# A new pace for the sample's gathered rows in both expert stages of a one-core encoder step: products, value sets, one row load and one copy stand at other places in the order

## The chip, the cores and the metric

The kernel runs on one core of one Trainium2 chip. The metric is device microseconds (us) of one launch; lower is better. Times of the profiled execution come from one trace. The engines are TensorE (PE: matmuls; PEld: its weight loads), VectorE (DVE), ScalarE (ACT), GpSimd (POOL, which here issues the gathers and a few row loads) and SyncE (SP, which issues the plain loads of the tables).

## The reference, cut to what matters

A two-layer encoder runs one step for a prompt of 256 frames and for a sample of 8 x 16 = 128 frames. Each layer is a mixer (a state-space scan in the first, windowed attention in the second) followed by `peer`, a retrieval over 16384 experts. The change is in `peer`:

```python
q = xn @ w_q                                   # 8 heads, two halves of 128
s1, s2 = q_half1 @ sub_k1.T, q_half2 @ sub_k2.T
...                                            # top 16 of each, top 16 of their sums
eid = e1 * 128 + e2                            # 8 x 16 = 128 experts a token
gate = softmax(vs)
ue = take(u_tab, eid)                          # (128 tokens, 128 experts, 1024)
act = gelu(einsum('tkd,td->tk', ue, x))
ve = take(v_tab, eid)
out = einsum('tk,tkd->td', gate * act, ve)
```

## The kernel before, in words

`peer(l)` runs twice, once for each layer. It treats the two token sets in different ways.

**The 256 prompt tokens go through all experts densely.** The tables `u_t` and `p_v` stream through once, a tile of 128 x 1024 f32 (512 KB) a step. There are 256 steps, which I number s = 0 to 255: s = 0 to 63 are the first half of u, s = 64 to 127 the second half, s = 128 to 255 the values v. In a u step (`u_step`) PE multiplies the tile with the prompt's activations, and ACT writes the result's GELU to `G[0]` or `G[1]`, a buffer of 64 expert columns for each half. Nearly every tile is split in two first (`split`): ACT rounds it (`hi`), DVE subtracts (`lo`), and PE makes three products of 8 matmuls (lines 144 to 146), 24 in a u step. A v step (`v_step`) has 12 matmuls of 512 columns (line 157), and its column of G is split as well (`phi`, `plo`). Some steps of the first half of u and of v run unsplit (lines 1188 and 1235). The gates are scattered into G by `w_step`, every second step from s = 64 to 191: DVE makes the masks `ob` (L1201), `og` (L1204) and half of `oa` (L1217), ACT the other half (L1214, L1215), PE does 16 small matmuls (L1221), and DVE multiplies the result into G (L1223).

**The 128 sample tokens fetch their own experts' rows.** There are 128 items in u. For each, POOL issues a gather of 512 KB (`fetch_u`, L1122) into one of three buffers `gath`, and DVE multiplies it with the tokens' rows and sums (`u_item`, L1160, called "the product" below). The products come in four groups of 32; each group needs the activations' rows in another arrangement, which `load_group(g)` (L946) brings from memory: groups 0 and 2 into the one buffer `xg`, groups 1 and 3 into columns of G that are free by then. A group's end (L1148, L1166) turns its 32 sums into coefficients. In v there are 32 sets of four rows: POOL gathers each row (`fetch_v`, L1122, into free columns of G), DVE makes a mask (`cm`, L1173) and PE adds the set with eight matmuls (`v_quad`, L1179), two for each of the four 32-column positions of the array.

**What sets the order.** All engines run their own instructions in a fixed order. A scheduler chooses it by its own simulated times when the kernel is built, and `pin` keeps some instructions in the order in which the code gives them. The code asks for the sample's work at each step: `tick(s)` makes products until as many are done as `U_DUE` wants by step s, with straight lines between its points, and for each it first fetches the row of the item after next; `quads(s)` makes the sets that `V_DUE` lists up to s, and then fetches rows for the next ones. `load_group(1)` stands at the turn of the halves (s = 64), `load_group(2)` behind item 31 and `load_group(3)` at v step 35 (s = 163). Before all this `peer` turns the normed activations and splits them (`qhi`, `qlo`), and ACT makes an unsplit copy `xf` (L931) for the unsplit steps.

Of the kernel before, what the change touches and what calls it, by code (L numbers as in the profile page):

```python
# [19 lines left out]
P = 128  # L20
# [35 lines left out]
U_DUE = ((64, 30), (128, 72), (192, 110), (216, P))  # L56
V_DUE = [72 + 7 * i for i in range(6)] + [148 + int(4.4 * i) for i in range(10)] + [193 + int(3.6 * i) for i in range(16)]
# [4 lines left out]
def encoder_step(ctx: ExitStack, tc: tile.TileContext, t_in, t_out):  # L62
# [825 lines left out]
    def peer(l):  # L888
        with ExitStack() as c:
# [35 lines left out]
            xf = T(xfctx.__enter__(), [P, KD, NP], F32, tag="xf")  # L925
            for k in range(KD):
                ps = bank([P, NT])
                for b in range(NB):
                    pe.transpose(ps[:, b * P:(b + 1) * P], xn[b][:, k * P:(k + 1) * P], ident)
                split(qhi[:, k], qlo[:, k], ps, scale=gcol[:, 2 + l, k:k + 1])  # L930
                act.activation(xf[:, k], ps[:, :NP], AF.Copy, scale=gcol[:, 2 + l, k:k + 1])  # L931
# [7 lines left out]
            def load_group(g):  # L939

                if g % 2:
                    xg[g] = (G[1][:, HE - 4:] if g == 1 else G[0][:, 32:36]).rearrange("p e t -> p (e t)")
                else:
                    xg[g] = T(one, [P, D], F32, tag="xg", bufs=1)
                rows = xrow[g]
                pool.dma_start(xg[g], bass.AP(tensor=rows.tensor, offset=rows.offset, ap=[[0, GR], [D, TG], [1, D]]))  # L946
# [184 lines left out]
            def fetch_v(n, s):  # L1131

                half, e = (1, HE - 20 + 4 * (n % 4)) if s < 2 * HE else (0, 4 * (n % v_bufs(s)))
                assert all(k != (half, e) for k, _ in vrows.values())
                tile_ = G[half][:, e:e + 4].rearrange("p e t -> p (e t)")
                r, q = divmod(n, 4)
                vrows[n] = (half, e), gather(tile_, t_in["p_v"], eidT[:, 32 * q + r:32 * q + r + 1])
# [17 lines left out]
            def u_item(k):  # L1155
                g, j = divmod(k, TG)
                if j == 0:
                    au[g] = T(one, [P, TG], F32, tag="au", bufs=1)
                tile_ = urows.pop(k)
                pin(dve.scalar_tensor_tensor(tile_, tile_, 1.0, xg[g], op0=OP.mult, op1=OP.mult,  # L1160
                                             accum_out=au[g][:, j:j + 1]))
                if j == TG - 1:
                    if g == 0:
                        load_group(2)
# [102 lines left out]
            def quads(s):  # L1267
# [8 lines left out]
                for _ in range(2):  # L1276
# [41 lines left out]
            for e2 in range(HE):  # L1318
# [4 lines left out]
                if e2 >= 4:  # L1323
                    quads(HE + e2)
# [5 lines left out]
            for e2 in range(2 * HE):  # L1330
                v_step(e2)
                if e2 == 35:
                    load_group(3)
# [127 lines left out]
```

## Time and profile before

| | us |
|---|---|
| three runs | 2552.58, 2550.56, 2542.86 |
| median | 2550.56 |
| the profiled execution, its own time | 2552.02 |
| its span, first to last instruction | 2550.1 |
| PE busy in the span | 2431.2 (95%) |
| DVE busy | 1883.9 (74%) |
| ACT busy | 1243.5 (49%) |
| POOL busy | 701.3 (27%) |

In the profiled execution `peer` of the first layer has its turn of the halves near 682 us, its v steps from about 919 to 1384 us. In the second layer the turn is near 1838 us, and the v steps run from about 2073 to 2536 us. A stretch's row gives the busy time of each engine there, the granted TensorE clock as a share of full speed, and the rate of the DMA engines. A row of the timeline gives start, length, engine, line, operation, tiles, and in brackets the engine's idle time ahead of it and what ended that.

### The profile page before, as it was taken

How to read it: one execution, taken by the hardware profiler on the slowest of the kernel's cores; microseconds unless marked ns; L12 is line 12 of the kernel's file. 1: busy time of each engine (PE TensorE's matmuls, PEld its weight loads, DVE VectorE, ACT ScalarE, POOL GpSimd, SP SyncE). 2: the span in 40 equal slices, each digit the busy share in tenths (PEclk: the TensorE clock that was granted, in tenths of full speed). 3: DMA queues.
4: the chain of work that ended last, by engine and by line, in shares of the span. 5: the costliest groups of instructions: out<-in, count | busy, mean ns of one | idle time of the engine just before them, and what ended most of it. 6: DMA issues, size and time to landing. Idle time of an engine off the chain costs nothing.

```text
span 2550.1 us, 44494 instructions
## 1 busy us (share of the span) xinstructions
PE 2431.2 (95%) x16655; PEld 2036.9 (80%) x16656; DVE 1883.9 (74%) x4163; ACT 1243.5 (49%) x2406; POOL 701.3 (27%) x755
## 2 busy tenths in 40 slices
PE   8999999999999999999999998999989999999998
PEld 7899978999888986656666878999978886656676
DVE  5888737979877788677655676978868787777655
ACT  5655524433555665554344554433546565554343
POOL 2222200022333224346432100022423224346431
PEclk9999999999999999999999999999989999999999
DMA  5545434477888889889996324477889889899995
GB/s 193 177 170 191 151 127 147 156 250 258 277 298 301 267 281 347 299 326 381 360 339 194 132 95 142 148 246 252 261 286 331 265 283 334 310 343 362 367 332 212
DMA packets 179768, 649.77 MB, mean 255 GB/s; under 512 B 23824, under 2 KB 25728, under 8 KB 176896
## 3 DMA queue, kind: packets, MB, share of 16 engines
q1 hardware_dynamic: 99936, 365.85, 41.0%
q0 software_dynamic: 79616, 281.08, 31.5%
q8 instruction: 130, 2.13, 0.3%
q14 instruction: 86, 0.70, 0.1%
HBM read 630.62 MB, written 18.06 MB: 254 GB/s over the span
## 4 chain that ended last, share of the span: by engine, by line
PE 75%; DVE 11%; DMA 6%; issue 4%; ACT 2%; POOL 1%; another core or an unknown queue 0%; SPq 0%; POOLq 0%; ACTq 0%; DVEq 0%
PE bank L157 25%; PE bank L146 10%; PE bank L144 10%; PE bank L145 10%; PE bank L1179 4%; DVE lo L109 3%; DMA gath<-in_p_u,eidU 3%; PE bank L1188 3%; PE bank L1235 3%; PE bank L1221 2%; DVE gath L1160 2%; DMA raw<-in_u_t 1%; ACT hi L108 1%; PE bank L504 1%; DMA h<-hd 1%
## 5 line engine op out<-in xcount | busy, mean ns | idle before, releaser
L108 ACT CAST hi<-raw 128x1024 fp32r<-128x1024 f32 (+1 forms) x479 | 497.3, 1040 | 574.6 <-PE bank L145 363.5
L109 DVE TENSOR_TENSOR lo<-raw,hi 128x1024 fp32r<-128x1024 f32 (+1 forms) x479 | 580.2, 1213 | 192.4 <-ACT hi L108 183.5
L1122 POOL DMA_INDIRECT gath<-in_p_u,eidU x256 | 305.5, 1194 | 961.3 <-DVE gath L1160 538.5
L146 PE MATMUL bank<-xhi,lo 128*128 128x256 f32 (+1 forms) x1344 | 412.6, 307 | 15.4 <-DVE lo L109 15.4
L144 PE MATMUL bank<-xhi,hi 128*128 128x256 f32 (+1 forms) x1344 | 410.9, 306 | 1.0 <-issue 0.5
L145 PE MATMUL bank<-xlo,hi 128*128 128x256 f32 (+1 forms) x1344 | 403.9, 301 | 0.0
L1122 POOL DMA_INDIRECT G<-in_p_v,eidT x256 | 284.8, 1113 | 301.6 <-PE bank L1179 225.9
L146 PEld LDWEIGHTS bank<-xhi,lo 128*128 128x128 f32 x1344 | 261.7, 195 | 23.3 <-DVE lo L109 19.0
L108 ACT CAST phi<-G 128x256 fp32r<-128x256 f32 x232 | 93.3, 404 | 372.0 <-PE bank L157 319.1
L144 PEld LDWEIGHTS bank<-xhi,hi 128*128 128x128 f32 x1344 | 262.1, 195 | 12.3 <-ACT hi L108 5.7
L145 PEld LDWEIGHTS bank<-xlo,hi 128*128 128x128 f32 x1344 | 261.5, 195 | 0.3
L144 PE MATMUL bank<-qhi,hi 128*128 128x256 f32 (+1 forms) x792 | 243.9, 308 | 9.0 <-ACT xf L931 7.4
L146 PE MATMUL bank<-qhi,lo 128*128 128x256 f32 (+1 forms) x792 | 238.3, 301 | 3.8 <-DVE lo L109 3.8
L145 PE MATMUL bank<-qlo,hi 128*128 128x256 f32 (+1 forms) x792 | 238.5, 301 | 0.0
L157 PE MATMUL bank<-hi,phi 128*128 128x512 f32 x640 | 203.8, 413 | 18.1 <-ACT phi L108 11.1
L109 DVE TENSOR_TENSOR plo<-G,phi 128x256 fp32r<-128x256 f32 x232 | 97.6, 422 | 152.6 <-PE bank L157 139.1
L157 PE MATMUL bank<-lo,phi 128*128 128x512 f32 x640 | 204.2, 399 | 4.6 <-DVE lo L109 4.3
L157 PE MATMUL bank<-hi,plo 128*128 128x512 f32 x640 | 201.4, 396 | 0.0
L1214 ACT ACTIVATE oa<-ioh,e2T 128x128 f16<-128x128 f16 x512 | 163.2, 390 | 74.4 <-PE bank L1221 64.7
L157 PEld LDWEIGHTS bank<-hi,phi 128*128 128x128 f32 x640 | 117.4, 190 | 79.5 <-ACT hi L108 19.0
L1160 DVE SCALAR_TENSOR_TENSOR gath<-gath,G 128x1024 f32<-128x1024 f32 x128 | 155.7, 1220 | 32.2 <-DMA gath<-in_p_u,eidU 20.5
L1160 DVE SCALAR_TENSOR_TENSOR gath<-gath,xg 128x1024 f32<-128x1024 f32 x128 | 155.4, 1214 | 23.1 <-DMA gath<-in_p_u,eidU 23.1
(361 smaller groups left out, 4891.8 us busy)
## 6 DMA issues: line engine op xcount, KB each, us to landing
raw<-in_u_t SPq DMA_DIRECT2D x256, 512.0 KB
raw<-in_p_v SPq DMA_DIRECT2D x256, 512.0 KB
raw<-in_w_in SPq DMA_DIRECT2D x32, 512.0 KB
raw<-in_p_w_q SPq DMA_DIRECT2D x32, 512.0 KB
raw<-in_w_z SPq DMA_DIRECT2D x16, 512.0 KB
s<-in_state_ssm SPq DMA_DIRECT2D x8, 1024.0 KB
out_sm_ssm<-s SPq DMA_DIRECT2D x8, 1024.0 KB
raw<-in_w_out SPq DMA_DIRECT2D x16, 512.0 KB
```

The costliest lines, as they stand in the source:

```text
L108: act.copy(hi, raw)
L109: dve.tensor_tensor(lo, raw, hi32, op=OP.subtract)
L144: pe.matmul(ps, whi[:, s], xhi[:, k, c0:c1], start=(k == 0), stop=False)
L145: pe.matmul(ps, whi[:, s], xlo[:, k, c0:c1], start=False, stop=False)
L146: pe.matmul(ps, wlo[:, s], xhi[:, k, c0:c1], start=False, stop=(k == KD - 1))
L157: mm = pe.matmul(ps, x, w[:, hf * n:(hf + 1) * n], start=s_, stop=e_)
L1122: pool.indirect_dma_start(out=tile_, out_offset=None, in_=tab, in_offset=bass.IndirectOffsetOnAxis(ap=idx, axis=0))
L1160: pin(dve.scalar_tensor_tensor(tile_, tile_, 1.0, xg[g], op0=OP.mult, op1=OP.mult, accum_out=au[g][:, j:j + 1]))
L1179: pin(pe.matmul(out_s[hf][32 * q:32 * q + 32, :], cm[:, q], rows[q][:, hf * 512:hf * 512 + 512], start=(r == 0), stop=(r == 31), tile_posi ...
L1188: pe.matmul(ps, raw[:, k * P:(k + 1) * P], xf[:, k], start=(k == 0), stop=(k == KD - 1))
L1214: act.activation(a[:, i], ioh, AF.Square, scale=-1.0, bias=e2T[:, t, 0:1])
L1235: pe.matmul(accs[b][hf], G[e2 // HE][:, e2 % HE, b * P:(b + 1) * P], raw[:, hf * 512:hf * 512 + 512], start=False, stop=False)
```

## The change

- The table of products' due steps is another. Between s = 64 and 70 hardly any is due now (30 are due at s = 63, 31 at s = 70), then 43 in the 57 steps up to s = 127 (before, 42 in 64 steps), 41 up to s = 191 (38), and the last 13 by s = 211 (18 by s = 215).
- The sets of values are due at 80, 85, ... (before 72, 79, ...), at 153 + 3.7 i (148 + 4.4 i) and at 194 + 3.9 i (193 + 3.6 i).
- `quads` fetches one row a step, two at every third step; before, two at each. It is first asked at e2 = 8 of u's second half, before at 4.
- `load_group(2)` is called at item 40, before it was behind item 31. `load_group(3)` is called at v step 20, before at 35, and puts its rows into columns 16 to 19 of `G[0]` instead of 32 to 35; the buffers of `fetch_v` leave these out.
- The copies `xf` are called one behind the second split and the other seven behind the loop; before, each behind its own split.

```diff
-U_DUE = ((64, 30), (128, 72), (192, 110), (216, P))
-V_DUE = [72 + 7 * i for i in range(6)] + [148 + int(4.4 * i) for i in range(10)] + [193 + int(3.6 * i) for i in range(16)]
+U_DUE = ((64, 30), (71, 31), (128, 74), (192, 115), (212, P))
+V_DUE = ([80 + int(5.4 * i) for i in range(6)] + [153 + int(3.7 * i) for i in range(11)]
+         + [194 + int(3.9 * i) for i in range(15)])
...
+            turned = []
+            def exact(k):
+                act.activation(xf[:, k], turned[k][:, :NP], AF.Copy, scale=gcol[:, 2 + l, k:k + 1])
             for k in range(KD):
                 ps = bank([P, NT])
+                turned.append(ps)
...
                 split(qhi[:, k], qlo[:, k], ps, scale=gcol[:, 2 + l, k:k + 1])
-                act.activation(xf[:, k], ps[:, :NP], AF.Copy, scale=gcol[:, 2 + l, k:k + 1])
+                if k == 1:
+                    exact(0)
+            for k in range(1, KD):
+                exact(k)
...
-                    xg[g] = (G[1][:, HE - 4:] if g == 1 else G[0][:, 32:36]).rearrange("p e t -> p (e t)")
+                    xg[g] = (G[1][:, HE - 4:] if g == 1 else G[0][:, 16:20]).rearrange("p e t -> p (e t)")
...
-                half, e = (1, HE - 20 + 4 * (n % 4)) if s < 2 * HE else (0, 4 * (n % v_bufs(s)))
+                k = n % (4 if s < 2 * HE else v_bufs(s))
+                half, e = (1, HE - 20 + 4 * k) if s < 2 * HE else (0, 4 * k + 4 * (k >= 4))
...
+                if k == TG + 8:
+                    load_group(2)
                 tile_ = urows.pop(k)
...
-                    if g == 0:
-                        load_group(2)
...
-                for _ in range(2):
+                for _ in range(1 if s % 3 else 2):
...
-                if e2 >= 4:
+                if e2 >= 8:
                     quads(HE + e2)
...
-                if e2 == 35:
+                if e2 == 20:
                     load_group(3)
```

Every engine has the same instructions before and after; only their order differs. In the rows below, line numbers of the changed kernel are those of its own file, which is some lines longer: L110 is the `lo` of L109, L1174 the product of L1160, L1235 the G of L1223, L1216 `og`, L1229 `oa`, L1213 `ob`, L158 the v matmul of L157, L1191 the set's matmul of L1179, L1133 a gather and L957 `load_group`.

On DVE, at the turn of the halves of the first layer, the kernel before has (`gath` <- `gath`, `xg` or `G_1193` is a product):

```order
L109 TENSOR_TENSOR lo_7291<-raw_7288,hi_7290 128x1024
L109 TENSOR_TENSOR lo_7323<-raw_7320,hi_7322 128x1024
L1160 SCALAR_TENSOR_TENSOR gath_7240,au_5426<-gath_7240,xg_4077 128x1024
L1223 SCALAR_TENSOR_TENSOR G_620_3971<-bank_7354,G_620_3971 128x64x8
L1204 TENSOR_TENSOR og_7458<-ob_7456,g_617_3965 128x1024
L1217 TENSOR_TENSOR oa_7474<-ioh_76,e2T_3964 128x512
L1201 TENSOR_TENSOR ob_7556<-ioh_76,e1T_3963 128x512
L109 TENSOR_TENSOR lo_7388<-raw_7385,hi_7387 128x1024
L109 TENSOR_TENSOR lo_7420<-raw_7417,hi_7419 128x1024
L1160 SCALAR_TENSOR_TENSOR gath_7276,au_5426<-gath_7276,xg_4077 128x1024
L1166 TENSOR_TENSOR cm_7453<-au_5426,same_q_82 128x128
L109 TENSOR_TENSOR lo_7489<-raw_7486,hi_7488 128x1024
```

The changed kernel has, five steps further on in the same place:

```order
L110 TENSOR_TENSOR lo_7417<-raw_7414,hi_7416 128x1024
L110 TENSOR_TENSOR lo_7479<-raw_7476,hi_7478 128x1024
L1235 SCALAR_TENSOR_TENSOR G_620_3971<-bank_7445,G_620_3971 128x64x8
L1216 TENSOR_TENSOR og_7542<-ob_7540,g_617_3965 128x1024
L1229 TENSOR_TENSOR oa_7558<-ioh_76,e2T_3964 128x512
L110 TENSOR_TENSOR lo_7511<-raw_7508,hi_7510 128x1024
L1213 TENSOR_TENSOR ob_7637<-ioh_76,e1T_3963 128x512
L1235 SCALAR_TENSOR_TENSOR G_620_3971<-bank_7539,G_620_3971 128x64x8
L1216 TENSOR_TENSOR og_7639<-ob_7637,g_617_3965 128x1024
L1229 TENSOR_TENSOR oa_7655<-ioh_76,e2T_3964 128x512
L110 TENSOR_TENSOR lo_7573<-raw_7570,hi_7572 128x1024
L1174 SCALAR_TENSOR_TENSOR gath_7240,au_5426<-gath_7240,xg_4077 128x1024
```

The product that reads `gath_7240` stood behind the second of these `lo` rows and stands now behind the seventh; the first product on group 1's rows (`G_1193`) stood three `lo` rows behind it and does so still.

On POOL, around the load of group 3 in the v steps (`G_620` <- `xrow`), the kernel before has:

```order
L1122 DMA gath_11759<-in_p_u,eidU_3962 128x1024
L1122 DMA G_620_3971<-in_p_v,eidT_3967 128x1024 x4
L1122 DMA gath_11851<-in_p_u,eidU_3962 128x1024
L946 DMA G_620_3971<-xrow_644_4072 128x1x1024
L1122 DMA gath_11930<-in_p_u,eidU_3962 128x1024
```

And the changed kernel:

```order
L1133 DMA G_620_3971<-in_p_v,eidT_3967 128x1024
L1133 DMA gath_11204<-in_p_u,eidU_3962 128x1024
L1133 DMA gath_11285<-in_p_u,eidU_3962 128x1024
L1133 DMA gath_11310<-in_p_u,eidU_3962 128x1024
L957 DMA G_620_3971<-xrow_644_4072 128x1x1024
L1133 DMA gath_11371<-in_p_u,eidU_3962 128x1024
```

The load stands about 15 steps earlier, and no four value rows in a run stand ahead of it any more.

On PE, in the second half of the v steps of the first layer, a set of eight matmuls stands in the kernel before as:

```order
L157 MATMUL bank_10538<-hix_13014,plo_13019 128x512
L157 MATMUL bank_10539<-hix_13014,plo_13019 128x512
L1179 MATMUL bank_7285<-G_620_3971,cm_13037 32x512 x4
L1179 MATMUL bank_7286<-G_620_3971,cm_13037 32x512 x4
L157 MATMUL bank_10536<-hi_13051,phi_13055 128x512
L157 MATMUL bank_10537<-hi_13051,phi_13055 128x512
```

And in the changed kernel, at nearly the same place:

```order
L158 MATMUL bank_10545<-hi_13068,plo_13073 128x512
L1191 MATMUL bank_7285<-G_620_3971,cm_13088 32x512
L158 MATMUL bank_10542<-hi_13101,phi_13105 128x512
L1191 MATMUL bank_7285<-G_620_3971,cm_13088 32x512
L158 MATMUL bank_10543<-hi_13101,phi_13105 128x512
L158 MATMUL bank_10542<-lo_13102,phi_13105 128x512
L158 MATMUL bank_10543<-lo_13102,phi_13105 128x512
L158 MATMUL bank_10542<-hi_13101,plo_13106 128x512
L158 MATMUL bank_10543<-hi_13101,plo_13106 128x512
L1191 MATMUL bank_7285<-G_620_3971,cm_13088 32x512
L158 MATMUL bank_10544<-hi_13101,phi_13105 128x512
```

The set's matmuls stand one by one between those of the dense step. In each layer the 32 sets stand in 37 unbroken runs before and in 51 after.

## Rows read from the trace of the kernel before

**Rows 1.** The page, parts 1 and 4: busy time; the chain by engine.

```profile
PE 2431.2 (95%) x16655; PEld 2036.9 (80%) x16656; DVE 1883.9 (74%) x4163; ACT 1243.5 (49%) x2406; POOL 701.3 (27%) x755
...
PE 75%; DVE 11%; DMA 6%; issue 4%; ACT 2%; POOL 1%; another core or an unknown queue 0%; SPq 0%; POOLq 0%; ACTq 0%; DVEq 0%
```

**Rows 2.** Stretches: length; busy PE, PEld, DVE, ACT, POOL; clock, DMA share, GB/s.

```profile
682.00:717.00 35.00, 27.23 (x224) 26.29 (x224) 19.62 (x31) 16.36 (x34) 11.25 (x10) 0.85 0.91 264
717.00:919.00 202.00, 195.55 (x1863) 182.19 (x1863) 161.93 (x248) 122.04 (x247) 55.99 (x56) 0.97 0.84 289
...
1832.00:1873.00 41.00, 32.09 (x266) 31.17 (x266) 22.63 (x35) 18.69 (x39) 13.51 (x12) 0.85 0.95 273
1873.00:2073.00 200.00, 194.17 (x1879) 180.73 (x1879) 162.08 (x248) 122.70 (x247) 55.47 (x56) 0.98 0.86 291
```

**Rows 3.** Timeline of POOL, turn of the halves, first layer.

```profile
680.41 0.74 POOL L946 DMA_DIRECT2D G<-xrow  x1 [1.73 <-ACT xlo L1300]
...
686.33 1.42 POOL L1122 DMA_INDIRECT G<-in_p_v,eidT  x1 [0.30 <-issue]
688.05 0.93 POOL L1122 DMA_INDIRECT gath<-in_p_u,eidU  x1 [0.30 <-issue]
```

**Rows 4.** Timeline of DVE, same place.

```profile
695.55 1.23 DVE L1160 SCALAR_TENSOR_TENSOR gath<-gath,G 128x1024 f32<-128x1024 f32 x1 [5.19 <-DMA G<-xrow]
...
708.76 1.23 DVE L1160 SCALAR_TENSOR_TENSOR gath<-gath,G 128x1024 f32<-128x1024 f32 x1 [6.29 <-DMA gath<-in_p_u,eidU]
```

**Rows 5.** Timeline of PE, same place, and the like in the second layer.

```profile
698.05 0.74 PE L1221 MATMUL bank<-og,oa 128*128 128x64 f16 x16 [3.31 <-DVE og L1204]
...
711.57 0.58 PE L146 MATMUL bank<-xhi,lo 128*128 128x256 f32 x1 [3.41 <-DVE lo L109]
...
1868.54 0.58 PE L146 MATMUL bank<-xhi,lo 128*128 128x256 f32 x1 [3.72 <-DVE lo L109]
```

**Rows 6.** The chain of waits: start, length, what; at the turn and in v.

```profile
688.05 20.68 DMA gath<-in_p_u,eidU
...
1042.32 18.82 DMA gath<-in_p_u,eidU
```

**Rows 7.** Timeline of DVE and PE behind the load of group 3, both layers.

```profile
1061.16 1.23 DVE L1160 SCALAR_TENSOR_TENSOR gath<-gath,xg 128x1024 f32<-128x1024 f32 x1 [6.39 <-DMA gath<-in_p_u,eidU]
...
1063.74 0.66 PE L1221 MATMUL bank<-og,oa 128*128 128x64 f16 x16 [3.24 <-DVE og L1204]
...
2216.80 0.65 PE L1221 MATMUL bank<-og,oa 128*128 128x64 f16 x16 [2.52 <-DVE og L1204]
```

**Rows 8.** Timeline of PE, an unbroken set of eight, and a lone matmul.

```profile
1088.60 1.92 PE L1179 MATMUL bank<-G,cm 128*32 128x512 f32 x16
1090.46 0.50 PE L157 MATMUL bank<-hi,plo 128*128 128x512 f32 x1
...
1107.80 1.04 PE L1179 MATMUL bank<-G,cm 128*32 128x512 f32 x2
1108.78 0.74 PE L157 MATMUL bank<-hix,phi 128*128 128x512 f32 x2
```

**Rows 9.** Timeline of PE, end of the gates' work in v, first layer.

```profile
1160.93 0.63 PE L1221 MATMUL bank<-og,oa 128*128 128x64 f16 x16 [0.35 <-DVE og L1204]
1163.65 0.67 PE L1221 MATMUL bank<-og,oa 128*128 128x64 f16 x16 [2.09 <-ACT oa L1215]
```

**Rows 10.** Timeline of PE: a wait in v's second half, and the first query matmul.

```profile
1220.26 1.18 PE L157 MATMUL bank<-hi,phi 128*128 128x512 f32 x4 [0.98 <-ACT hi L108]
...
398.10 0.69 PE L144 MATMUL bank<-qhi,hi 128*128 128x384 f32 x1 [3.83 <-ACT xf L931]
```

**Rows 11.** Stretches, columns as in rows 2: end of u; second half of v.

```profile
867.00:919.00 52.00, 52.00 (x524) 51.04 (x520) 47.79 (x76) 35.75 (x74) 10.51 (x11) 1.00 0.81 265
1167.00:1247.00 80.00, 76.10 (x359) 52.02 (x360) 52.57 (x82) 28.49 (x43) 46.47 (x39) 0.98 1.01 398
```

**Rows 12.** Timeline of PE, a wait amid u's second half, first layer.

```profile
781.54 0.95 PE L1221 MATMUL bank<-og,oa 128*128 128x64 f16 x16 [2.05 <-DVE og L1204]
```

## The prediction

> **What bounds the kernel now.** I read the page's busy times first, then the chain by engine. PE is busy 95% of the span and holds 75% of the chain; DVE, at 74%, holds 11% [rows 1]. So a PE matmul added in a full stretch costs its whole length, and a wait removed is worth something only where PE itself waits. I then read stretches of `peer`. At the end of u's second half PE is busy in every one of 52.00 us; around the turn of the halves it is busy 27.23 of 35.00 us in the first layer, 32.09 of 41.00 in the second, at a granted clock of 0.85, against 0.97 and 0.98 behind it [rows 2, 11]. The turn is the one place with much to win. The timelines tell what ends the waits there. POOL issues group 1's rows, four value rows and then a gather, with nothing between [rows 3]; DVE waits 5.19 us for the first of these and 6.29 us for the last, which took 20.68 us from issue on [rows 4, 6]; PE waits 3.31 and 3.41 us for what DVE has queued behind these two products, `og` and `lo` [rows 5]. The second layer shows the same with 3.72 us [rows 5]. The same form returns once in v, at the load of group 3: DVE waits 6.39 us for a gather of 18.82 us, PE 3.24 and, in the second layer, 2.52 us [rows 6, 7].
>
> **The change part by part.** The sum is made on the profiled execution, 2552.0 us.
>
> *The stop at the turn.* The order of DVE has seven `lo` ahead of the product that had two, so the products on group 1's rows come five steps, some 15 us, later, while the loads stay where POOL had them. That is more than the 5.19 and 6.29 us that DVE waited, so both waits should go. What they cost: in the first layer PE was idle 35.00 - 27.23 = 7.77 us; at the idle share of the stretch behind, (202.00 - 195.55) / 202.00 = 3.2%, it would be 1.1, so 6.7 us are the turn's. Its 27.23 us of work ran at a clock of 0.85, not 0.97: 27.23 x (1 - 0.85 / 0.97) = 3.4 us more. Together 10.1 us. In the second layer: 41.00 - 32.09 = 8.91, less 41 x 2.9% = 1.2, is 7.7; 32.09 x (1 - 0.85 / 0.98) = 4.3; together 12.0 us [rows 2]. The burst of six transfers is still there and still delays the plain loads of u's tiles; for that I leave 1 us a layer. **-20 us**; the ends are -22 (nothing left) and -10 (PE waits for the tiles instead).
>
> *The load of group 3* now stands between gathers of u, with the value rows one by one instead of four in a run ahead of it. The wait there was 3.24 + 2.52 us [rows 7]. **-6 us**; at worst it is the same wait 15 steps earlier, 0. Group 2's load waits for `xg` as before and is needed much later: nothing.
>
> *The sets of values on PE.* This is the term that speaks against the change. A set is eight matmuls, two on each column position. Unbroken it takes 1090.46 - 1088.60 = 1.86 us; one lone matmul of a set takes 1108.78 - 1107.80 = 0.98 us [rows 8]. So four positions run beside one another, and what counts is how many times the same position comes again: two rounds are 1.86 us, one round 0.98, whether it holds one matmul or four. In the order the sets of one layer stand in 37 runs before: 32 with two rounds, 5 with one. After the change they stand in 51: 33 with two, 18 with one. 32 x 1.86 + 5 x 0.98 = 64.4 us become 33 x 1.86 + 18 x 0.98 = 79.0 us: 14.6 us more a layer. Nothing hides it, since PE is what the stretch waits for; **+29 us** for both layers. It could be half of that where a lone matmul falls into a wait of PE, as the 0.98 us ahead of a dense step in v's second half [rows 10]; I take the whole, because PE is busy 76.10 of 80.00 us there [rows 11].
>
> The Trainium skill ("TensorE: Matmul & The Clock Gate", section "Measured speedup vs the span model") gives for small tiles of the array set side by side a speedup of 3.07 for four row tiles and of 2.38 for three column tiles, so that four together take 4 / 3.07 = 1.30 times one. By that a lone matmul would be 0.93 / 1.30 = 0.71 us and the term an estimated 22 us, the total 7 us lower; the trace shows 0.98 us for the lone one and 0.93 for a round of four, so the trace speaks against it here.
>
> *The end of the gates' work in v.* The order of PE has two groups of `w_step` closely one behind the other there before, four after, since the sets moved. Such a step from one to the next cost PE 0.35 and 2.09 us [rows 9], 1.2 in the mean; two more are 2.4 us a layer: **+5 us**, between +1 and +8.
>
> *The second half of v.* The wait of 0.98 us for ACT's `hi` [rows 10] stands four times in each layer; the order that leads to it (ACT makes two `phi` in a row ahead of `hi`) stands about twice after. 2 x 2 x 0.98: **-4 us**, with 0 as the other end.
>
> *DVE and the gathers at the new pace.* Products are due at 43 in 57 steps instead of 42 in 64, 0.754 a step against 0.656: 0.098 x 1.23 us [rows 4] = 0.12 us of DVE more a step. At the end of u DVE is busy 47.79 of 52.00 us, in some 16.5 steps (524 matmuls, 48 and the gates' 16 in two steps), so 3.15 us a step; with 16.5 x 0.12 = 2.0 it is at 96% [rows 11]. PE still sets the pace on average, with less to spare: I take 1 us a layer, **+2 us**, between 0 and +8. The DMA engines move more there than before, at 265 GB/s and a share of 0.81; v's second half shows 398 GB/s [rows 11], so I cost the rate itself at nothing.
>
> *The copies `xf`.* In both orders all eight stand in a row behind the eight roundings of `qhi` on ACT, so the first query matmul waits its 3.83 us as before [rows 10]. Nothing.
>
> Sum: -20 - 6 + 29 + 5 - 4 + 2 = +6, so 2558 us for an execution like the profiled one. This lies 1.5 us above the median of the runs shown; I predict 2557 us: a gain at the turn that the broken sets eat up.
>
> **The rivals.** *The gain stays (2529 us).* The turn gives its whole 22 us and group 3 its 6; the broken sets cost half, +14.6, as lone matmuls fall where PE waits anyway; no loss at the end of the gates' work; -4 in v's second half; and the wait of 2.05 us amid u's second half [rows 12], which has the same releaser `og` behind products, goes in each layer, -4. -22 - 6 + 15 - 4 - 4 = -21 or -22, less 1.5. For it speaks that waits and lone matmuls both stand ahead of dense steps in the new order; against it that PE has few waits left to fill.
>
> *The gathers come too late (slower, 2583 us).* A gather is issued when the product three items back has freed its buffer. At the new pace of 0.754 a step that is some four steps of 3.15 us, 12.6 us, ahead of its use. Where a burst is on its way a gather takes 18.8 to 20.7 us [rows 6]. The mechanism decides wherever landing takes over 12.6 us: DVE then stands 6 us, PE about 3 [rows 7]. If the denser pace brings that four more times a layer, it is 8 x 3.24 = 26 us: 2558 + 26 - 1.5 = 2583. Its place is v's first half, where value rows, gathers and group 3's load come together. Against it: in the first layer's u the lead was hardly longer and PE ran without any wait at the end of u [rows 11].
>
> *The change does not do what it says (2551 us).* For the copies the order shows that. For the turn it would need DVE's stop to be filled by other waiting, such as `lo` on late tiles, just as long, and the sets' breaks to be free.
>
> **How the numbers follow.** About 0.5% (12.8 us, so 2538 to 2563) is what a measurement of this kernel tells from no change. Chances: my forecast 0.45 (of it 0.37 within, 0.06 above, 0.02 below), the gain stays 0.24, the gathers come too late 0.24, no effect 0.07. That is faster 0.26, same 0.44, slower 0.30. The range goes from the one rival to the other, 2529 to 2583: what is beyond them at both ends, half of each rival's cases at most, is about 0.2. The forecast's own range is 2545 to 2567, from the ends of the turn and of the sets.
>
> **What would show it.** Right: the stretch of 35 us around the turn at an idle share and clock as behind it; no wait of DVE above 2 us on group 1's rows or the gather behind; no wait of PE on `og` at group 3's load; the set's line on PE about 15 us busier a layer, with lone rows of about 1 us between dense ones. Wrong: PE waiting for `lo` on late tiles at the turn (its gain is lost), DVE waiting for gathers in v's first half (the slower rival), or a lone set matmul that is much shorter than 0.98 us (the faster one).

## The result, and the profile after

| | before | after |
|---|---|---|
| median, us | 2551.57 (4 runs, 2542.86 to 2558.28) | 2585.95 (4 runs, 2576.72 to 2587.85) |
| ratio after to before | | 1.0126, 95% interval 1.0098 to 1.0153 |
| profiled execution, its own time | 2552.02 | 2576.72 |
| span | 2550.1 | 2575.0 |

The change makes the kernel slower by 1.3%, outside the range of the prediction (2529 to 2583) and on the side of its slower rival, though not by that rival's mechanism. The profiled execution of the changed kernel is its fastest one; its three other runs lie 9 to 11 us higher, and no trace of those says why. What follows explains the 24.7 us between the two profiled executions. Experiments are given as ratios to the kernel before on the same chip, since chips differ by about 1%: the runs were taken on three occasions, each on one chip, on which the kernel before has medians of 2547, 2526 and 2523 us. A ratio of one chip need not hold for another, since most of such a difference lies in u's second half, as is shown under "Same rows, or form?".

The page of the changed kernel, parts 1 and 4, answers to [rows 1]. PE is busy 29.5 us longer (2431.2 before), DVE and ACT as long as before:

```profile
PE 2460.7 (96%) x16655; PEld 2038.0 (79%) x16656; DVE 1885.0 (73%) x4163; ACT 1245.7 (48%) x2406; POOL 703.0 (27%) x755
...
PE 64%; DVE 9%; DMA 5%; issue 4%; ACT 2%; POOL 1%; another core or an unknown queue 1%; POOLq 0%; SPq 0%; DVEq 0%; ACTq 0%
```

I cut both traces at the same events: the first matmul with `xhi` (u's second half), the first with `phi` (v), the last one of `w_step` (v's second half) and the last with `plo`. The stretches of the first layer, kernel before first (columns as in [rows 2]: length; busy PE, PEld, DVE, ACT, POOL; clock, DMA share, GB/s):

```profile
678.19:923.82 245.63, 229.81 (x2162) 215.22 (x2160) 188.22 (x289) 145.65 (x295) 69.96 (x69) 0.95 0.86 287
923.82:1164.32 240.50, 232.81 (x1400) 154.48 (x1400) 186.05 (x317) 129.63 (x260) 101.81 (x86) 0.99 0.90 322
1164.32:1388.54 224.22, 215.39 (x1033) 150.84 (x1033) 129.66 (x190) 90.48 (x134) 84.39 (x90) 0.99 0.89 328
```

And the changed kernel:

```profile
676.04:925.06 249.02, 231.81 (x2162) 212.93 (x2160) 190.07 (x293) 145.09 (x295) 71.31 (x70) 0.96 0.85 286
925.06:1169.65 244.59, 237.18 (x1402) 155.15 (x1402) 190.02 (x323) 130.07 (x260) 106.06 (x90) 0.99 0.90 332
1169.65:1401.77 232.12, 223.57 (x1032) 150.62 (x1031) 124.15 (x179) 91.05 (x134) 78.92 (x85) 0.99 0.82 298
```

Every stretch grew: by 3.4, 4.1 and 7.9 us here, by 3.8, 4.2 and 1.9 us in the second layer, 25.3 us in all. In both v stretches PE's busy time grew with the length. U's second half did not get shorter, which is the surprise: PE is idle 15.8 us there before and 17.2 us after, and the clock, 0.95 and 0.96, is hardly better. The expected gain at the turn is not there.

**The turn.** Group 1's rows do land within the stop now. On DVE the first product on them, which waited 5.19 us before [rows 4], follows without a wait at 705.53. But 20 us later a wait of the old kind stands there (rows of POOL, DVE and PE in the timeline of the changed kernel; the last row is the second layer):

```profile
704.97 0.74 POOL L957 DMA_DIRECT2D xg<-xrow  x1
...
705.53 1.23 DVE L1174 SCALAR_TENSOR_TENSOR gath<-gath,G 128x1024 f32<-128x1024 f32 x1
...
707.04 0.98 POOL L1133 DMA_INDIRECT gath<-in_p_u,eidU  x1 [1.33 <-DVE gath L1174]
...
726.14 1.22 DVE L1174 SCALAR_TENSOR_TENSOR gath<-gath,G 128x1024 f32<-128x1024 f32 x1 [6.66 <-DMA gath<-in_p_u,eidU]
...
724.56 0.39 PE L145 MATMUL bank<-xhi,hi 128*128 128x256 f32 x1 [1.52 <-ACT hi L109]
729.83 0.58 PE L147 MATMUL bank<-xhi,lo 128*128 128x256 f32 x1 [4.77 <-DVE lo L110]
...
1900.48 0.58 PE L147 MATMUL bank<-xhi,lo 128*128 128x256 f32 x1 [4.49 <-DVE lo L110]
```

The gather that DVE waits for was issued behind `xg <- xrow`, the load of group 2, and took from 707.04 to 726.14, though no burst of value rows goes ahead of it. So a single load of a group is enough. The kernel before issued this load too, 0.9 us behind the gather that waited [rows 3] (its timeline):

```profile
688.98 0.74 POOL L946 DMA_DIRECT2D xg<-xrow  x1
```

So at its turn there were two loads, at 680.41 and 688.98, with five gathers between them. What a load does is seen in stretches behind the loads of group 1 and group 2 in the changed kernel:

```profile
682.00:692.00 10.00, 9.65 (x92) 9.35 (x91) 6.07 (x7) 5.82 (x12) 1.74 (x2) 1.00 1.01 239
710.00:722.00 12.00, 12.00 (x125) 11.87 (x125) 7.83 (x14) 4.91 (x11) 1.91 (x2) 1.00 1.03 208
```

The DMA engines are shown as busy all the time (1.01, 1.03), yet they move 239 and 208 GB/s, where v's second half before moved 398 at the same share [rows 11]. Behind a load of 512 KB the rate is 52% to 60% of that, for ten us and more.

**The sets.** Their line on PE, before and after:

```profile
L1179 PE MATMUL bank<-G,cm 128*32 128x512 f32 x1024 | 134.5, 603 | 0.0
```

```profile
L1191 PE MATMUL bank<-G,cm 128*32 128x512 f32 x1024 | 166.7, 606 | 2.4 <-DMA G<-in_p_v,eidT 1.8 <-issue 0.6
```

The same 1024 records take 32.2 us more of PE. A part of a set between dense matmuls costs what the lone one cost [rows 8]:

```profile
1043.34 1.05 PE L1191 MATMUL bank<-G,cm 128*32 128x512 f32 x4 [1.28 <-DMA G<-in_p_v,eidT]
1044.32 0.50 PE L158 MATMUL bank<-lo,phi 128*128 128x512 f32 x1
```

Two matmuls (four records) take 0.98 us, the same as one, and about the same as a round of four (half of 1.86 us).

### The profile page after: what moved, and what is told of

It is laid out like the page before. It is cut to its first block, busy times and chain, and to the rows that moved or that the text cites. A ratio compares the mean times of both kernels' runs of the same rounds, so it can differ in the third digit from the quotient of the medians.

```text
span 2575.0 us, 44514 instructions
## 1 busy us (share of the span) xinstructions
PE 2460.7 (96%) x16655; PEld 2038.0 (79%) x16656; DVE 1885.0 (73%) x4163; ACT 1245.7 (48%) x2406; POOL 703.0 (27%) x755
## 4 chain that ended last, share of the span: by engine, by line
PE 64%; DVE 9%; DMA 5%; issue 4%; ACT 2%; POOL 1%; another core or an unknown queue 1%; POOLq 0%; SPq 0%; DVEq 0%; ACTq 0%
PE bank L158 23%; PE bank L147 9%; PE bank L145 8%; PE bank L146 8%; PE bank L1191 5%; PE bank L1200 3%; DVE lo L110 3%; PE bank L1247 3%; DMA gath<-in_p_u,eidU 2%; PE bank L1233 2%; DVE gath L1174 1%; ACT hi L109 1%; DMA raw<-in_u_t 1%; DMA G<-in_p_v,eidT 1%
## 5 line engine op out<-in xcount | busy, mean ns | idle before, releaser
L109 ACT CAST hi<-raw 128x1024 fp32r<-128x1024 f32 (+1 forms) x479 | 496.8, 1040 | 571.5 <-PE bank L146 350.7
L110 DVE TENSOR_TENSOR lo<-raw,hi 128x1024 fp32r<-128x1024 f32 (+1 forms) x479 | 580.7, 1214 | 194.2 <-ACT hi L109 192.0
L1133 POOL DMA_INDIRECT gath<-in_p_u,eidU x256 | 306.8, 1199 | 932.5 <-DVE gath L1174 507.3
L1133 POOL DMA_INDIRECT G<-in_p_v,eidT x256 | 284.9, 1113 | 368.0 <-PE bank L1191 285.6
L109 ACT CAST phi<-G 128x256 fp32r<-128x256 f32 x232 | 93.3, 405 | 376.8 <-PE bank L158 324.2
L110 DVE TENSOR_TENSOR plo<-G,phi 128x256 fp32r<-128x256 f32 x232 | 97.5, 422 | 160.8 <-PE bank L158 154.0
L158 PE MATMUL bank<-hi,phi 128*128 128x512 f32 x640 | 202.4, 411 | 9.2 <-ACT phi L109 7.2
L158 PE MATMUL bank<-lo,phi 128*128 128x512 f32 x640 | 202.9, 397 | 4.3 <-DVE lo L110 4.2
L158 PE MATMUL bank<-hi,plo 128*128 128x512 f32 x640 | 200.6, 395 | 0.0
L1174 DVE SCALAR_TENSOR_TENSOR gath<-gath,G 128x1024 f32<-128x1024 f32 x128 | 155.9, 1221 | 25.4 <-DMA gath<-in_p_u,eidU 24.9
L1174 DVE SCALAR_TENSOR_TENSOR gath<-gath,xg 128x1024 f32<-128x1024 f32 x128 | 155.4, 1214 | 24.9 <-DMA gath<-in_p_u,eidU 24.8
L158 PEld LDWEIGHTS bank<-hi,phi 128*128 128x128 f32 x640 | 117.8, 189 | 68.8 <-issue 19.0
```

Of the source, the lines that this page charges most:

```text
L109: act.copy(hi, raw)
L110: dve.tensor_tensor(lo, raw, hi32, op=OP.subtract)
L158: mm = pe.matmul(ps, x, w[:, hf * n:(hf + 1) * n], start=s_, stop=e_)
L1133: pool.indirect_dma_start(out=tile_, out_offset=None, in_=tab, in_offset=bass.IndirectOffsetOnAxis(ap=idx, axis=0))
```

## Experiments

Two theories, with a rival each. **Theory 1:** the broken sets cost PE their length. Rival: they fill time in which PE waits anyway. **Theory 2:** each load of a group slows all DMA traffic for some 12 us, and the load of group 2 now comes out of the stop. Rival: the denser pace of products makes the gathers late.

**Sets kept whole.** In the changed kernel the matmuls of the dense v steps keep the code's order too, so that most sets stand whole (70 rounds a layer instead of 84):

```diff
-                        if len(terms) > 1:
-                            pin(mm)
+                        pin(mm)
```

> The changed kernel, with the matmuls of the v steps kept in the order of the code among those of the sets, so that most sets of eight stand unbroken again: 70 rounds of column positions a layer instead of 84. Theory 1 (the broken sets cost PE their whole length): 14 rounds x 0.93 us x 2 layers = 26 us less than the changed kernel, about 2560 us, a ratio of 1.003 to the kernel before, and PE's busy time on the sets' line falls from 166.7 to about 140 us. Rival (lone matmuls fill time in which PE waits anyway, so the slowdown comes from elsewhere): the sets' line falls as much but the time stays within 8 us of the changed kernel's 2586.

Measured: ratio 1.0061 (1.0039 to 1.0084), 17 us below the changed kernel's 1.0126 (26 were expected, under 8 by the rival); the profiled executions, of two occasions, differ by 24 us (2552.8 against 2576.7). PE's busy time fell from 2460.7 to 2428.1 us, 20 of these 33 us in the sets' line. Theory 1 holds, with a rest: the sets' line fell only to 146.6 us instead of 140, and PE now waits for the last rows of whole sets. The waits of PE, summed over this run (engine, line, what it waits for: us, times, longest):

```profile
PE bank L1190 <- DMA G<-in_p_v,eidT: 10.1, 6, 2.3
```

**No load of group 2** in the changed kernel; its products read group 0's rows, so this transfer is left out:

```diff
                 if k == TG + 8:
-                    load_group(2)
+                    xg[2] = xg[0]
```

> The changed kernel without the load of group 2 (its products read group 0's rows, so this load's 512 KB a layer are left out). Theory 2 (the load itself makes the gathers behind it late, and has moved out of the stop): DVE's wait of 6.7 us for a gather and PE's waits of 1.5 and 4.8 us near 724 to 730 us, and 4.5 us near 1900, vanish, with some 3 us of half clock behind each: 14 to 17 us less than the changed kernel, ratio to the kernel before near 1.006. Rival (the denser pace of products, with three buffers, makes the gathers late): a wait of DVE of 4 us or more for a gather stays within 40 us behind the turn, and the time falls by under 5 us.

Measured: ratio 1.0064 (1.0040 to 1.0087), 16 us below the changed kernel. The stretch of u's second half, first layer:

```profile
678.12:913.63 235.51, 225.60 (x2162) 207.84 (x2160) 189.80 (x293) 145.10 (x295) 70.86 (x69) 0.99 0.88 301
```

It is 13.5 us shorter than in the changed kernel (249.02), idle time 9.9 instead of 17.2 us, clock 0.99. On the same chip the run with whole sets, which has this load, gives both layers:

```profile
678.45:926.66 248.21, 230.53 (x2162) 212.32 (x2160) 190.21 (x293) 145.20 (x295) 70.80 (x71) 0.97 0.86 287
1835.28:2078.13 242.85, 227.32 (x2162) 208.68 (x2160) 189.87 (x293) 145.21 (x295) 72.75 (x71) 0.99 0.88 294
```

Without the load the two stretches are 235.51 and 237.41 us, 18 us shorter in all, which is about the 16 us of the time. DVE's only wait for a gather there is one of 0.76 us. Theory 2, not the pace.

**Why is a load slow?** It reads the same 32 rows four times in one transfer. Two runs of the kernel *before* ask whether that matters: one writes the rows to memory four times, so that a load reads 512 KB in a row; the other reads 128 other rows of the table of u.

```diff
-            xrow = T(dram, [GR, 4, RG, D], F32, tag=f"xrow{l}")
-            for c4 in range(4):
-                sync.dma_start(xrow[:, c4], xn[2][32 * c4:32 * c4 + 32])
+            xrow = T(dram, [GR, GR, 4, RG, D], F32, tag=f"xrow{l}")
+            for q in range(GR):
+                for c4 in range(4):
+                    sync.dma_start(xrow[:, q, c4], xn[2][32 * c4:32 * c4 + 32])
...
-                ... ap=[[0, GR], [D, TG], [1, D]]))
+                ... ap=[[D, P], [1, D]]))
```

> The kernel before, with the sample's rows written to memory four times (2 MB instead of 0.5 MB a layer, ahead of the query matmuls) so that a load of a group reads 512 KB of distinct addresses instead of the same 128 KB four times. Theory 3 (what makes a load slow is that it reads the same rows four times): the DMA engines keep 350 to 400 GB/s behind each load instead of 220 to 240 at the same busy share; DVE's waits of 5.2 and 6.3 us at the turn and 6.4 us in v shrink to under 2 us each; 15 to 26 us less than before, ratio 0.990 to 0.994. Rival (any load of this form on this queue, or simply the number of transfers in the burst, is slow): the rate stays at 220 to 240 GB/s there, ratio 0.998 to 1.003.

> The kernel before, with the loads of the groups reading 128 other rows in a row of the table of u instead of the sample's own rows (so the sample's products are of other numbers): the same form and bytes, no row read twice, and a memory region that nobody has written. Theory 3: as with the copied rows, 350 to 400 GB/s behind each load and no wait of DVE above 2 us at the turn. Rival (the form of the load): 220 to 240 GB/s and DVE's waits of 5 to 6 us as before. If this one is fast and the copied rows are not, it is where the rows lie, not how often they are read.

Measured: ratio 0.9856 (0.9826 to 0.9886) with the rows copied, 34 us below before, which is more than the 15 to 26 expected; where the rest comes from was not followed. The other rows, one run, 2507.91 us. The stretches behind the two loads at the turn, kernel before and then with the rows copied:

```profile
686.00:698.00 12.00, 8.73 (x85) 8.43 (x83) 6.04 (x10) 5.78 (x11) 5.24 (x6) 1.00 1.03 306
698.00:708.00 10.00, 9.23 (x81) 9.02 (x81) 4.47 (x7) 4.45 (x9) 0.00 (x0) 0.83 1.00 242
```

```profile
686.00:698.00 12.00, 12.00 (x125) 11.86 (x124) 10.40 (x16) 7.91 (x18) 5.68 (x6) 1.00 0.98 375
698.00:708.00 10.00, 10.00 (x96) 9.78 (x95) 8.36 (x15) 6.04 (x13) 2.62 (x2) 1.00 1.00 381
```

With the other rows it is 381 and 380 GB/s. The burst of six transfers is the same, and PE is busy throughout: the loss at the turn lay in how these loads read. Which of the two loads held up which gather is not told apart, since both changed.

**Same rows, or form?** The two runs changed both: no address twice, and a source in two steps instead of three. So one run reads the same 128 KB four times, but in four plain transfers of 32 rows; the other keeps the three-step form on four copies that lie eight rows apart.

```diff
-                pool.dma_start(xg[g], bass.AP(..., ap=[[0, GR], [D, TG], [1, D]]))
+                for q in range(GR):
+                    pool.dma_start(xg[g][q * TG:(q + 1) * TG], bass.AP(..., ap=[[D, TG], [1, D]]))
```

> The kernel before, with each load of a group written as four plain loads of 32 rows: the same 128 KB are still read four times, but no single transfer repeats its source. Theory 3a (the repeated source in one transfer is what is slow, a matter of its form): packets under 512 B fall from 23824 to about 20850 as with the copied rows, the rate behind a load is 350 to 400 GB/s, ratio to before 0.984 to 0.990. Theory 3b (reading the same memory rows four times within a few us is slow): the rate stays at 220 to 240 GB/s and the ratio at 0.997 to 1.003.

> The kernel before, with the rows written to memory four times and a gap of eight rows behind each copy, so that a load reads distinct addresses, yet has the three-step form of the kernel before. Theory 3a (form): 220 to 240 GB/s behind a load, DVE's waits of 5 to 6 us at the turn, about 23800 packets under 512 B, about 2550 us. Theory 3b (the same rows): 350 to 400 GB/s, no wait of DVE above 2 us on group 1's rows, about 2513 us.

Measured: four plain loads 0.9881 (0.9857 to 0.9905); copies with gaps 2526.13 us in one run, where the kernel before has a median of 2526.08. It is the form. With the gaps DVE waits at the turn as before:

```profile
694.86 1.23 DVE L1161 SCALAR_TENSOR_TENSOR gath<-gath,G 128x1024 f32<-128x1024 f32 x1 [5.69 <-DMA G<-xrow]
708.62 1.23 DVE L1161 SCALAR_TENSOR_TENSOR gath<-gath,G 128x1024 f32<-128x1024 f32 x1 [6.85 <-DMA gath<-in_p_u,eidU]
```

and 224 GB/s move in the ten us from 698 on (348 with four plain loads).

This run also shows where the occasions differ. It has the order and the slow form of the kernel before, but is from the chip where that one has a median of 2526; its two stretches of u's second half are:

```profile
676.98:908.86 231.88, 222.67 (x2162) 209.51 (x2160) 188.30 (x289) 145.61 (x295) 71.31 (x69) 0.98 0.89 304
1822.10:2057.76 235.66, 222.57 (x2162) 209.39 (x2160) 188.39 (x289) 145.58 (x295) 71.77 (x69) 0.96 0.89 299
```

The kernel before in its own trace has 245.63 and 244.64 there, so 23 of the 26 us between the two spans (2550.1 and 2524.4) lie in u's second half, some 10 of them idle time and some 10 a lower clock. The waits of PE at the turn are about as long in both (16.0 and 18.5 us, both layers); the small waits of over 0.3 us behind the turn, 11.6 us in the kernel before, are missing here. No run tells why.

The packets on the page, in order: before, four plain loads, copies with gaps.

```profile
DMA packets 179768, 649.77 MB, mean 255 GB/s; under 512 B 23824, under 2 KB 25728, under 8 KB 176896
```

```profile
DMA packets 177081, 649.77 MB, mean 260 GB/s; under 512 B 21136, under 2 KB 23040, under 8 KB 174208
```

```profile
DMA packets 180633, 652.93 MB, mean 259 GB/s; under 512 B 23920, under 2 KB 25824, under 8 KB 177760
```

The slow form makes some 2700 more small packets in eight loads. The Trainium skill has a rule that fits ("DMA: Bandwidth & Descriptors", section "Rules for kernel authors"): a transfer whose outermost step has a small count c, such as a leading repeat of c copies, runs on at most c of the 16 DMA engines. Here c is 4, and 32 in the plain loads. The runs agree that the form decides, with 4 copies of distinct rows as slow as 4 repeats; no view here shows the single DMA engines, and the mean share of 1.0 over all of them does not by itself look like four at work.

**The change with fast loads.** The changed kernel with the rows copied as above:

> The changed kernel with the rows copied as in the run that had them copied in the kernel before (2513 us). With slow loads out of both, what is left between the two is the sets' breaks and the pace. Theory 1 with the sets' breaks alone: 15 rounds x 0.93 x 2 = 28 us, of which the run with whole sets gave back 17 to 22 for 14 rounds: 2531 to 2541 us, ratio to before 0.993 to 0.998. Rival (the even pace is worth something by itself): under 2528 us; rival (the denser pace makes gathers late): over 2545 us.

Measured: 0.9998 (0.9984 to 1.0011), 2524.2 us; the kernel before with four plain loads, on the same chip, 2494.6. Both have fast loads (in two forms), and the change costs 30 us of median and 24 us between the profiled executions; their PE busy times in the six stretches differ by 25 us (1360.49 against 1335.44). u's second half, first layer:

```profile
679.44:903.77 224.33, 221.95 (x2163) 205.72 (x2161) 190.05 (x293) 145.42 (x295) 73.46 (x71) 1.00 0.90 318
```

PE is idle 2.4 us and the clock is 1.00: the denser pace costs nothing there, so the rival to theory 2 falls a second time. What is left of the change is the sets: their line is 166.6 us here and 133.5 with four plain loads. As a ratio the run missed its expectation, 0.993 to 0.998, and lies beyond the bound of the slower rival (2545 us are 0.999 of the 2547 on which it was reckoned). But DVE's waits for gathers, which that rival needs, sum up to 24.2 us over this run and to 32.3 with four plain loads in the kernel before, so they did not grow.

**The kernel before with copied rows and whole sets**

> The kernel before with the rows copied and the sets' matmuls kept whole: 64 rounds a layer instead of 69. Theory 1: 5 x 0.93 x 2 = 9 us below the kernel with the rows copied alone, about 2504 us, ratio to before 0.983. Rival (whole sets make PE wait for the value rows where a broken set began while its last rows were on their way): 2510 to 2518 us, with new waits of the sets for value rows.

Measured: 0.9855 (0.9831 to 0.9878), 2487.25 us, the lowest of all runs; on the same chip four plain loads alone gave 0.9881. The 7 us between them fit 5 rounds a layer, but the intervals overlap, and the copied rows alone had the same ratio on another chip (0.9856). 0.983 was expected, and as a ratio the rival's band begins at 0.985, so the time decides nothing. The sets' line fell from 133.5 to 125.3 us, with 1.5 us of new waits for value rows.

**Which edit breaks the sets** needed no run; the order of PE's matmuls tells it. In the kernel before with the stop alone it is 71 rounds, with the stop and the new pace of u 72, with the new due steps of the sets alone 82, with both 84. The new due steps in v do it (3.7 instead of 4.4 steps apart in the first half, 3.9 instead of 3.6 in the second).

**The stop alone** in the kernel before (and the six sets in u due from 80 on, which the stop forces):

```diff
-U_DUE = ((64, 30), (128, 72), (192, 110), (216, P))
+U_DUE = ((64, 30), (71, 31), (128, 72), (192, 110), (216, P))
-V_DUE = [72 + 7 * i for i in range(6)] + ...
+V_DUE = [80 + int(5.4 * i) for i in range(6)] + ...
```

> The kernel before with only the stop of the products at the turn (30 due at s = 63, 31 at s = 70, then as before) and the six sets of u's second half due from 80 on, as the change has them, since a set can't come before its coefficients. Sets in v as before: 71 rounds a layer instead of 69. Theory 2 (the stop covers group 1's slow load, and group 2's, which follows product 31, comes out of it and makes the same wait later): idle time of PE and half clock in u's second half as in both kernels, some 50 us for both layers; with 2 x 0.93 x 2 = 4 us for the sets the ratio is 0.998 to 1.004. Rival (the prediction's step: the stop takes 20 us away): ratio 0.991 to 0.995.

Measured: 0.9989 (0.9971 to 1.0007). The kernel gains nothing that can be told from zero, and the wait is there again (DVE, PE):

```profile
724.08 1.23 DVE L1160 SCALAR_TENSOR_TENSOR gath<-gath,G 128x1024 f32<-128x1024 f32 x1 [9.30 <-DMA gath<-in_p_u,eidU]
...
726.50 0.58 PE L146 MATMUL bank<-xhi,lo 128*128 128x256 f32 x1 [6.66 <-DVE lo L109]
```

The sets' line is 137.9 us, 3.4 more than in the kernel before, so the stop itself gives an estimated 6 us (2 to 11 by the interval), not 20. But the sign that theory 2 named, some 50 us of idle time and lower clock in u's second half, is not there. Both layers:

```profile
676.04:908.27 232.23, 222.96 (x2162) 207.83 (x2160) 187.25 (x288) 145.06 (x295) 71.41 (x69) 0.98 0.90 303
1817.78:2048.58 230.80, 222.91 (x2163) 207.68 (x2161) 187.20 (x288) 145.03 (x295) 71.90 (x69) 0.99 0.89 305
```

Idle time and lower clock are 23 us here. The 50 us are those of the first two traces; there is no trace of the kernel before from this chip. The nearest, the copies with gaps on a chip of nearly the same median, has 31 us. By these two traces, too, the stop takes some 8 us, and the wait behind the load of group 2 is what stays.

**Both loads in the stop.** The changed kernel with group 0 finished before the turn, so that both slow loads are issued as the stop begins:

```diff
-U_DUE = ((64, 30), (71, 31), (128, 74), (192, 115), (212, P))
+U_DUE = ((64, 32), (71, 33), (128, 74), (192, 115), (212, P))
-                if k == TG + 8:
+                if k == TG:
                     load_group(2)
```

> The changed kernel, with all 32 products of group 0 due before the turn and the stop behind them, so that the loads of groups 2 and 1 are issued one behind the other at its beginning, in the slow form of the kernel before. Sets as in the changed kernel (84 rounds). Theory 2: the stop now covers both slow loads; idle time and half clock in u's second half fall from 49 us (both layers) to the 25 us that were left without the load of group 2; 16 to 24 us less than the changed kernel, ratio to before 1.003 to 1.007. Rival (two slow loads together outlast the stop): waits of 4 to 6 us stay behind the turn, ratio 1.010 or more.

Measured: 1.0097 (1.0063 to 1.0131), above the 1.003 to 1.007 expected. The trace shows the waits of theory 2 gone, and others in their place. From the turn to the end of u DVE waits for no gather any more, only 1.58 us for group 1's rows (1.82 in the second layer), and u's second half is 229.66 us long with 6.8 us of idle time:

```profile
689.08:918.74 229.66, 222.90 (x2163) 207.40 (x2161) 187.14 (x287) 145.38 (x295) 69.37 (x68) 0.99 0.91 307
```

But the products that had to come earlier make PE wait ahead of the turn, 5.24 us in the first layer and 3.34 in the second:

```profile
665.25 0.58 PE L147 MATMUL bank<-qhi,lo 128*128 128x256 f32 x1 [5.24 <-DVE lo L110]
```

As a time this run is inconclusive: its interval overlaps the changed kernel's, which is of another occasion.

**Both prices taken out, in both kernels** (four plain loads, sets whole; 66 rounds a layer in the kernel before, 70 in the changed one):

> The kernel before with each load as four plain ones and the sets kept whole: 66 rounds a layer instead of 69. By theories 1 and 3a: 3 x 0.93 x 2 = 6 us below the run with four loads alone (ratio 0.988), that is 0.985 to 0.987. Rival (keeping sets whole makes PE wait for value rows): 0.988 or more.

> The changed kernel with both of its prices taken out: four plain loads for each group, sets kept whole (70 rounds a layer; 66 in the kernel before with the same two edits, which runs on the same chip). If the pace itself is worth nothing, it is 4 x 0.93 x 2 = 7 us slower than that one, a ratio 0.003 higher. If the even pace helps by itself it is equal or faster; if it starves DVE of gathers it is more than 12 us slower.

Measured: 0.9872 (0.9836 to 0.9908) and 0.9924 (0.9897 to 0.9950). The first lies between its expectation and its rival. Even without both prices the change costs 13 us, where 7 were expected from the four rounds. The sets' line shows the rest, first before, then changed:

```profile
L1180 PE MATMUL bank<-G,cm 128*32 128x512 f32 x1024 | 129.4, 599 | 1.0 <-DMA G<-in_p_v,eidT 1.0
```

```profile
L1192 PE MATMUL bank<-G,cm 128*32 128x512 f32 x1024 | 144.0, 603 | 10.6 <-DMA G<-in_p_v,eidT 10.6
```

It is busy for 14.6 us more, twice the four rounds, and PE waits 9.6 us more for value rows; other waits are shorter. By its 13 us the run falls where DVE was to starve of gathers (over 12 us), but DVE does not: its waits for them are 12.6 us in the changed kernel and 28.1 in the one before. What comes late is the value rows. They are fetched one a step, two at every third, with sets that are due 3.7 steps apart. In the changed kernel as it stands PE waits only 1.8 us for them. I take it that its sets begin with the rows that are there, so that the breaks and the late rows are two forms of one price; this is argued, not shown. That the fetching, and not the due steps, makes the rows late was not run.

## Why the prediction was wrong, step by step

- **The stop at the turn: -20 us predicted, about -2 measured.** This is the step that failed. Idle time and the time lost to a lower clock (PE's busy time in each stretch of 4 us, times what the granted clock lacks to 1) in u's second half were 15.8 + 10.3 + 16.3 + 8.4 = 51 us over both layers before and 17.2 + 7.4 + 16.7 + 7.8 = 49 us after. Of this the waits of PE at the turn itself went from 16.0 to 11.5 us, while the small waits further on grew from 11.6 to 16.6 us. The prediction read the waits at the turn as those of a burst of six transfers. They were those of the slow loads in that burst and right behind it: with fast loads the same burst makes no such wait. It set group 2's load at nothing because its rows are needed late. But that load waits for product 31, the last that reads `xg`, which the stop moves to its own end; in POOL's order it stands right behind that product, though the code calls it at item 40 now. So it came out behind the stop and held up the gathers there. The price of moving it was not in when its data is used, but in what it does to the transfers behind it. Without it, on one chip, u's second half is 18 us shorter over both layers, nearly the whole term.
- **The load of group 3: -6 predicted.** The waits of 3.24 and 2.52 us [rows 7] are gone; waits for value rows of 1.28 and 0.52 us stand in v's first half now, and one of 1.42 us for `lo`. About -2 or -3. DVE still waits 6.48 and 4.79 us for a gather behind this load; PE feels little of it.
- **The sets: +29 predicted, +32.2 measured** as busy time of PE; the rounds of column positions, 0.98 and 0.93 us, were the right measure.
- **End of the gates' work: +5 predicted, +2 measured.** Four waits of PE from 1158 to 1172 us sum up to 6.7 us in the first layer, five to 7.5 in the second; before it was 5.9 and 6.0.
- **v's second half: -4 predicted, about -1 measured.** Four waits of 0.98 us are there in the first layer, three in the second.
- **DVE and gathers at the new pace: +2 predicted.** With fast loads it is 0 in u, where PE is idle 2.4 us. In the changed kernel's own trace the small waits behind the turn are 5 us more, as said above; whether that is the pace stays open. The price of the pace is in v, with the sets.
- **The copies `xf`: 0 predicted.** PE waits 3.6 us for them in the changed kernel, before 3.83 [rows 10].

With the turn at -2 instead of -20 the sum is +24, and the profiled executions differ by 24.7. This close fit is partly luck: the terms as measured sum up to some +29, and about 4 us of small waits amid v's first half, near 1132 and 2284 us in the kernel before, are gone, for which the prediction had no term. The median lies higher by another 10 us; that part is not explained.

The slower rival gave a time near the measured one, 2583, but not by its mechanism. Its sign did show in v's first half: DVE's waits for gathers there grew from 18.5 to 29.0 us over both layers. But PE's idle time there did not grow (14.7 us before, 14.2 after); what made the time were the sets and the load of group 2.

## What to carry to other kernels

When a wait is named after the last of several transfers, ask which one of them slowed the others: here a DMA share of 1.0 at little more than half the usual GB/s was the sign of a transfer in a poor form, and mending its form (four plain loads instead of one with a repeat, -1.2%) was worth more than the new pace around it. A load that waits for a step goes along when that step is moved, and its price is what stands behind it, however late its data is needed. Where small matmuls share the array by column position, count the rounds in the order of the engine, since a set that is broken amid a round pays a full round more.

## What the runs showed of the hardware

- A transfer of 512 KB in three steps with an outermost count of four went along with 208 to 242 GB/s of all DMA traffic for 10 to 12 us, and a gather behind it took 19 to 21 us; with the same bytes as one block or as four plain transfers it was 348 to 381 GB/s in the two stretches at the turn. Whether the four blocks were the same rows or distinct ones made no difference.
- One or two matmuls of 512 columns on different column positions of the array took the same 0.98 us; a set of eight, two on each of four positions, took 1.86, so 0.93 a round.
- Chips differed: the kernel before had medians of 2547, 2526 and 2523 us on three occasions, each on one chip. Between the trace of the kernel before and one of the same load form from the chip of 2526, 23 of 26 us lay in one stage, u's second half (one trace each; chip and occasion are not told apart).
